# Scores as four products with corrections, k-interleaved starts, later norm statistics and decay copies on ScalarE in a two-layer decoder trunk

## The chip, the cores and the metric

The kernel runs on one core of a Trainium2 chip. The time is the device time of one launch in microseconds (us); runs of the kernel before and of the changed one are compared by their medians. The engines are called TensorE (PE in the rows, PEld its weight loads), VectorE (DVE), ScalarE (ACT), GpSimd (POOL) and SyncE (SP, which here only starts transfers).

## The reference

One inference step of a two-layer trunk on 592 columns: 16 meta tokens, 64 sample tokens (8 sequences of 8) and 512 prompt tokens, with a model width of 1024. Each layer is a mixer and an MLP, each followed by a layer norm. The even mixer runs a state space part (SSD, 16 heads) and a gated recurrence (RG-LRU) side by side; the odd one runs 4 GLA heads and 8 HGRN2 heads. Cut to what the change touches:

```python
# layer norm after each mixer and each MLP
mu = mean(x);  var = mean(square(x - mu))
y = (x - mu) * rsqrt(var + eps) * g + b
# convolution before SSD and RG-LRU, four taps
out = b + sum(full[:, t:t + L] * w[t] for t in range(4))
# SSD, per chunk of 64: decay from cumulated log a
decay = exp(where(causal, b[t] - b[s], -inf))
y_intra = einsum(cb * decay, xd)
# GLA and HGRN2, per chunk c of 64, b = cumsum(log_f)
b_ref = b[:, c // 2]
scores = einsum('tk,sk->ts', q * exp(b - b_ref), k * exp(b_ref - b))
scores = where(causal, scores, 0);  o_intra = scores @ v
S = S * exp(b_last) + (k * exp(b_last - b)).T @ v
# MLP
y = square(relu(h @ w1)) @ w2
```

The kernel takes the GLA and HGRN2 chunks in pairs of 128 tokens, so that one tile of scores holds two reference chunks on its diagonal and one block between them.

## The kernel before

**Tiling.** Activations lie transposed, features on the 128 partitions and the 592 columns along the free axis, cut into two halves of 296 (after the second layer's mixer 288, since the meta columns are dropped). A dense product of 1024 by 1024 is eight k-tiles of 128 by 128 weights for each output tile. For precision each operand is a high and a low fp32r part, and each k-tile costs three matmuls (`mm`, L176 to L186): 24 matmuls for one half of one output tile. Weight tiles come from memory in order; ScalarE casts the high part (L126) and VectorE subtracts the low one (L127). Products of the MLP's second matrix use a two-by-two scheme with fewer multiplications (L195).

**Order.** The program is written as one sequence of `Task`s (L276). A task makes its two halves, its `consume` takes the result out of PSUM, and after each half `weave` (L265) takes every generator in `active` one step further: state space pairs (`pair`, L832), heads (`attend`, L1150) and norms are such generators, so that their small products stand between the large ones. A function in `later[k]` runs after k-tile k of the next product (L184). A scheduling layer then fixes the order on each engine, and each engine works through its own queue in that order. PSUM has five banks for dense products (`pm`) and three for small ones (`px`).

**Norm.** `Norm.add` (L431) takes a finished tile of the residual, squares it on ScalarE and adds it into a sum of squares on VectorE (L447), and the tile itself into a plain sum (L444, the last tile's on VectorE). `finish` puts the statistics of half 0 into `later[FIK]`, with FIK 3, so the two matmuls with a matrix of ones (L463, L465) follow k-tile 3 of the next product; those of half 1 come at once, after `drain`. `finishing` subtracts the mean, scales and writes the high and low part of the next stage's input `h` (L494 to L496).

**Stage starts.** Each MLP starts with four output tiles half by half (`run(..., by_half=True)`, L648), the odd mixer with a 32-wide product for the GLA decay (`lr`), then q, k, v0 and v1 (L1404).

**State space pair.** The convolution has its first tap on VectorE (L706), two more there (L708), the last at L781; ScalarE takes a tanh (L783) and VectorE makes `xs` (L787). `pair` loads its states (`sin`), makes `rr` and `rx`, the per-head log decays spread over masks, on GpSimd (L843, L845), and after steps in between multiplies them into decays on TensorE (L879, L884), exponentiates (L881, L885), and builds inter-chunk outputs and states (L894 to L929).

**Head.** `attend` makes four exponentials of cumulated decays: `e1` (queries), `kx` (keys against the middle of a chunk), `e4` (keys to the chunk's end) and `e3`. Scores of a pair of chunks are two products of 64 query columns (L1265, L1266), the second with keys referred to another point. Then come the 32-wide products of the sample tokens with the states (L1276).

Of the kernel before, what the change touches and what calls it, by code (L numbers as in the profile page):

```python
# [14 lines left out]
P = 128  # L15
# [11 lines left out]
FIK = 3  # L27
# [44 lines left out]
def _trunk(ctx, tc, nc, I, O):  # L72
# [221 lines left out]

    def run(tasks, by_half=False, after=None):
# [99 lines left out]
    class Norm:  # L395
# [3 lines left out]
        def __init__(self, new, rs, halves, gname, bname, layer, final=False):  # L399
            self.rs, self.halves, self.final = rs, halves, final  # L400
            self.gname, self.bname, self.layer = gname, bname, layer
            self.new = new

# [27 lines left out]
        def add(self, k, i):  # L431
# [15 lines left out]
            V.tensor_tensor(ss, ss, q, OP.add)  # L447

        def finish(self, i, dst):
            if i == 0:  # L450
                later.setdefault(FIK, []).append(lambda: step(self.finishing(i, dst)))
            else:
                drain()
                for _ in self.finishing(i, dst):
                    pass

        def finishing(self, i, dst):
            c0, c1 = self.halves[i]
# [88 lines left out]
    def mlp(H, layer, halves, last, keep=None):  # L547
# [3 lines left out]
        with ExitStack() as st:  # L551
# [96 lines left out]
            run([w1(0, f) for f in W1_ORDER[:4]], by_half=True)  # L648
# [27 lines left out]
    def even_mixer(H, g):  # L676
# [10 lines left out]
        def conv_task(i, w, b, done):  # L687
# [3 lines left out]
            def consume(p, c0, c1, half):  # L691
# [14 lines left out]
                V.tensor_scalar(acc[:, 0:OW], t[:, 0:OW], w(0), b, OP.mult, OP.add)  # L706
# [125 lines left out]
        def pair(j, xs, zs, gs):  # L832
# [9 lines left out]
            for i, l in enumerate((lah.bitcast(F32), lal.bitcast(F32))):  # L842
# [6 lines left out]
            yield  # L849
            xd = s2.tile([P, 5, 2, 64], F32, tag="xd", name="xd")  # L850
# [270 lines left out]
    def odd_mixer(H, g):  # L1121
# [28 lines left out]
        def attend(q, k, ls, sc, qs, vf, gate, gcol, sdram, sout, pout, more):  # L1150
# [18 lines left out]

            kx = sd.tile([P, 64 + 4 * 192], F32, tag="kx", name="kx")  # L1170
            kc = kx[:, 64:].rearrange("p (c r s) -> p c r s", c=4, r=3)
# [6 lines left out]
            V.tensor_tensor(kc[:, :, 1], b4[:, :, 96:97].to_broadcast([P, 4, 64]), b4[:, :, 0:64], OP.subtract)  # L1178
            c = slice(16, 592)
            A.activation(kx[:, 0:64], e1[:, 16:80], AF.Exp, scale=-sc)  # L1180
            A.activation(kc[:, :, 0:3:2], e1[:, 80:592].rearrange("p (c r s) -> p c r s", c=4, r=2), AF.Exp, scale=-sc)
            A.activation(e1[:, c], e1[:, c], AF.Exp, scale=sc)
            A.activation(e4, e4, AF.Exp, scale=sc)
            A.activation(kc[:, :, 1], kc[:, :, 1], AF.Exp, scale=sc)
# [14 lines left out]
            k4 = k[:, 80:592].rearrange("p (c r s) -> p c r s", c=4, r=2)  # L1199
            V.tensor_tensor(kx[:, 0:64], k[:, 16:80], kx[:, 0:64], OP.mult)  # L1200
            V.tensor_tensor(kc[:, :, 0:2], k4[:, :, 0:1].to_broadcast([P, 4, 2, 64]), kc[:, :, 0:2], OP.mult)
            V.tensor_tensor(kc[:, :, 2], k4[:, :, 1], kc[:, :, 2], OP.mult)
            V.tensor_tensor(e4, k, e4, OP.mult)
            for j in range(2):
# [55 lines left out]

            p = px()
# [8 lines left out]
            p = px()  # L1270
            if nv == 2:
                samples(p[:, 256:512])
# [350 lines left out]
```

## Time and profile before

| | before |
|---|---|
| median of 3 runs | 1928.42 us (1928.1 to 1928.71) |
| profiled execution | 1926.06 us, span 1924.3 us |
| TensorE busy | 1858.2 us, 97% |
| VectorE busy | 1297.1 us, 67% |
| ScalarE busy | 886.0 us, 46% |
| GpSimd busy | 417.2 us, 22% |
| granted TensorE clock, mean | 0.987 |
| chain that ended last | PE 80%, DVE 13%, ACT 3%, issue 3% |

A share of busy time is a mean over stages with different limits. By the clock of the span, the state space part fills about 0 to 260 us, RG-LRU 260 to 380, the first output product and norm to 485, the first MLP to 893, the odd mixer to 1420, its output product and norm to 1510, the second MLP to 1908, and the last norm and stores the rest. "Idle" of an instruction is the time that its engine stood still just before it, and the arrow names what ended that. PEclk is the clock granted to TensorE as a share of its full 2.4 GHz; 0.50 is its other level, 1.2 GHz.

### The profile page before, as it was taken

The page shows a single profiled execution, that of the slowest core. Times are in us where ns is not written, and L with a number is a line of the kernel's source. Part 1 is how long each engine was busy: PE and PEld are TensorE (multiplying, and loading weights), DVE is VectorE, ACT ScalarE, POOL GpSimd, SP SyncE. Part 2 cuts the span into 40 slices and gives each one's busy share as a digit, 9 for nine tenths or more (in the row PEclk, how much of TensorE's full clock was granted, in tenths as well). Part 3 has the DMA queues.
Part 4 walks back from the last instruction along what each step waited for, and adds up shares of the span by engine and source line. Part 5 has one row for each costly group of instructions (what it writes and reads, how often), then busy time and mean ns, then how long its engine had stood idle before and what let it go on. Part 6 is the DMA issues. An engine that isn't in the chain of part 4 may idle for free.

```text
span 1924.3 us, 33593 instructions
## 1 busy us (share of the span) xinstructions
PE 1858.2 (97%) x13854; PEld 1819.0 (95%) x13854; DVE 1297.1 (67%) x2035; ACT 886.0 (46%) x1550; POOL 417.2 (22%) x435
## 2 busy tenths in 40 slices
PE   8998899999999999998999999999999999999996
PEld 8998799899999999998999999999999999999996
DVE  7997766877975756549645465665755976666647
ACT  5333246623644444324644455665732653534333
POOL 2554432214100000035422222221203200000024
PEclk9999899999999999999999999999999999999998
DMA  6232221421213131322332233223231214141311
GB/s 205 91 114 72 75 100 47 132 88 47 87 56 120 46 127 48 122 76 72 132 113 104 100 104 106 84 90 102 91 126 56 77 56 132 46 131 55 122 55 50
DMA packets 68761, 175.97 MB, mean 91 GB/s; under 512 B 6624, under 2 KB 30304, under 8 KB 67456
## 3 DMA queue, kind: packets, MB, share of 16 engines
q1 hardware_dynamic: 67968, 171.40, 26.5%
q8 instruction: 109, 1.79, 0.4%
q0 software_dynamic: 640, 2.43, 0.4%
q14 instruction: 44, 0.36, 0.1%
HBM read 154.54 MB, written 19.25 MB: 90 GB/s over the span
## 4 chain that ended last, share of the span: by engine, by line
PE 80%; DVE 13%; ACT 3%; issue 3%; POOL 0%; DMA 0%; SPq 0%; ACTq 0%; DVEq 0%; POOLq 0%
PE pm L182 55%; PE pm L195 14%; DVE w L127 1%; DVE r L424 1%; DVE h L496 1%; DVE r L494 1%; PE px L1326 1%; DVE r L478 1%; PE px L1337 1%; PE px L1336 1%; PE px L1067 1%; DVE lnq L447 1%; DVE acc L708 1%; PE px L925 1%; DVE ln L447 1%
## 5 line engine op out<-in xcount | busy, mean ns | idle before, releaser
L182 PE MATMUL pm<-h,w 128*128 128x296 f32 (+2 forms) x8256 | 1178.2, 301 | 11.0 <-ACT h L308 5.4
L182 PEld LDWEIGHTS pm<-h,w 128*128 128x128 f32 x8256 | 1132.6, 189 | 22.6 <-ACT h L308 5.4
L127 DVE TENSOR_TENSOR w<-raw,w 128x1024 fp32r<-128x1024 f32 (+1 forms) x300 | 369.7, 1233 | 165.1 <-ACT w L126 164.5
L126 ACT CAST w<-raw 128x1024 fp32r<-128x1024 f32 (+1 forms) x300 | 304.2, 1015 | 301.6 <-PE pm L195 152.2
L195 PE MATMUL pm<-ff,w 128*128 128x296 f32 (+1 forms) x2016 | 273.3, 297 | 0.0
L195 PEld LDWEIGHTS pm<-ff,w 128*128 128x128 f32 x2016 | 271.9, 188 | 0.1
L620 POOL TENSOR_TENSOR sq<-sq 128x296 f32<-128x296 f32 (+1 forms) x32 | 21.5, 674 | 651.4 <-ACT sq L618 651.4
L182 PE MATMUL pm<-m,w 128*128 128x296 f32 (+1 forms) x768 | 108.2, 304 | 0.0
L182 PE MATMUL pm<-ff,w 128*128 128x296 f32 (+1 forms) x768 | 108.0, 303 | 0.0
L182 PEld LDWEIGHTS pm<-m,w 128*128 128x128 f32 x768 | 106.8, 194 | 0.8 <-issue 0.3
L182 PEld LDWEIGHTS pm<-ff,w 128*128 128x128 f32 x768 | 106.6, 193 | 0.8 <-issue 0.3
L607 DVE TENSOR_TENSOR ff<-sq,ff 128x888 fp32r<-128x888 f32 (+3 forms) x48 | 58.4, 1221 | 42.1 <-ACT ff L606 42.1
L588 ACT ACTIVATE sq<-pm 128x296 f32<-128x296 f32 (+1 forms) x96 | 37.9, 414 | 87.0 <-PE pm L182 66.0
L606 ACT CAST ff<-sq 128x888 fp32r<-128x888 f32 (+3 forms) x48 | 50.3, 1050 | 39.6 <-DVE sq L601 38.9
L1361 POOL TENSOR_TENSOR o<-o,zs 128x576 f32<-128x576 f32 x16 | 31.3, 1967 | 148.7 <-DVE o L1360 148.7
L1280 POOL TENSOR_TENSOR sin<-sin,ebl 128x1024 f32<-128x1024 f32 (+1 forms) x12 | 35.8, 2980 | 106.1 <-issue 101.2
L211 DVE TENSOR_TENSOR r<-r,pm 128x296 f32<-128x296 f32 (+1 forms) x96 | 43.5, 453 | 18.6 <-PE pm L195 18.0
L589 ACT ACTIVATE sq<-sq 128x296 f32<-128x296 f32 (+1 forms) x96 | 41.2, 450 | 0.8
L1366 ACT COPY v<-pm 128x296 f32<-128x296 f32 x32 | 12.9, 405 | 58.6 <-PE pm L182 58.6
L214 DVE TENSOR_TENSOR r<-r,pm 128x296 f32<-128x296 f32 (+1 forms) x72 | 32.6, 452 | 10.2 <-PE pm L195 10.2
L618 ACT ACTIVATE sq<-pm 128x296 f32<-128x296 f32 (+1 forms) x32 | 13.0, 414 | 56.8 <-PE pm L182 53.8
L495 ACT ACTIVATE h<-r,vec 128x296 fp32r<-128x296 f32 (+1 forms) x48 | 23.8, 536 | 31.5 <-DVE r L494 31.5
(390 smaller groups left out, 2261.3 us busy)
## 6 DMA issues: line engine op xcount, KB each, us to landing
raw<-in_w_dram SPq DMA_DIRECT2D x252, 512.0 KB, 3.3
sin<-in_sst_dram SPq DMA_DIRECT2D x8, 512.0 KB, 3.7
out_ssd_s_dram<-sin SPq DMA_DIRECT2D x8, 512.0 KB, 3.1
sin<-in_gst_dram SPq DMA_DIRECT2D x4, 1024.0 KB, 5.7
out_gla_s_dram<-sin SPq DMA_DIRECT2D x4, 1024.0 KB, 3.9
sin<-in_hst_dram SPq DMA_DIRECT2D x8, 512.0 KB, 4.4
out_hgrn_s_dram<-sin SPq DMA_DIRECT2D x8, 512.0 KB, 3.5
xt<-in_x_dram SPq DMA_DIRECT2D x16, 148.0 KB, 4.2
```

The costliest lines, as they stand in the source:

```text
L126: A.copy(w[:, 0, :n], r)
L127: V.tensor_tensor(w[:, 1, :n], r, w[:, 0, :n].bitcast(F32), OP.subtract)
L182: PE.matmul(p[:, :n], w[:, a, ks], xs[k][:, b, c0:c1], start=(k == 0 and i == 0), stop=(k == KT - 1 and i == 2))
L195: PE.matmul(p[:, :n], w[:, a, ks], xs[k][:, b, :n], start=(first and k == 0 and i == 0), stop=(k == 3 and i == 2), skip_group_check=True)
L211: V.tensor_tensor(y, y, p[:, :n], OP.add)
L214: V.tensor_tensor(y, y, p[:, :n], OP.subtract)
L447: V.tensor_tensor(ss, ss, q, OP.add)
L588: A.activation(q, p, AF.Relu)
L589: A.activation(q, q, AF.Square)
L606: A.copy(t[:, 0, a:e, :n], s[:, a + 1:e + 1, :n])
L607: V.tensor_tensor(t[:, 1, a:e, :n], s[:, a + 1:e + 1, :n], t[:, 0, a:e, :n].bitcast(F32), OP.subtract)
L1280: G.tensor_tensor(sin, sin, ebl[:, 0:8].unsqueeze(2).to_broadcast([P, 8, N]), OP.mult)
```

## The change

Seven edits:

1. FIK is 6, so the statistics of half 0 come three k-tiles, nine matmuls, later in the next product.
2. `together` takes up to four tasks through the k-tiles side by side, one PSUM bank each: at the start of an MLP, and at the start of the odd mixer, where `lr`, q, k and v0 share one run.
3. The addition of a square into the sum of squares is put off until the next tile comes (`add_square`).
4. Half 1's `finish` prepares one more weight unit ahead of `drain`.
5. The first tap of the convolution goes from VectorE to ScalarE (20 times).
6. The spread log decays of a pair go from four GpSimd instructions to twenty ScalarE copies with a per-partition scale, eight before the first `yield` of the pair and twelve after.
7. The scores of a head are four products of 128 query columns with one set of keys, and four 64 by 64 ones that write the second chunk's own upper block anew with keys of the other reference point; the transposes of the samples come ahead of them, and key exponentials and products are fewer and longer.

```diff
-FIK = 3
+FIK = 6
...
+    def together(tasks, i):
+        ps = []
+        for t in tasks:
+            if t.small is None and t.w is None:
+                t.w = next_unit()
+            ps.append(pm())
+        for k in range(KT):
+            ks = slice(k * P, (k + 1) * P)
+            for t, p in zip(tasks, ps):
+                c0, c1 = t.halves[i]
+                if t.small is not None:
+                    ops = [(p[:32], t.small[:, k, :], b) for b in range(2)]
+                else:
+                    ops = [(p, t.w[:, a, ks], b) for a, b in ((0, 0), (0, 1), (1, 0))]
+                for j, (o, w, b) in enumerate(ops):
+                    PE.matmul(o[:, :c1 - c0], w, t.xs[k][:, b, c0:c1], start=(k == 0 and j == 0),
+                              stop=(k == KT - 1 and j == len(ops) - 1))
+            for fn in later.pop(k, ()):
+                fn()
...
-            V.tensor_tensor(ss, ss, q, OP.add)
+            self.add_square()
+            self.square = (ss, q)
...
+                prep_to(state["use"] + 4)
                 drain()
...
-            run([w1(0, f) for f in W1_ORDER[:4]], by_half=True)
+            ts = [w1(0, f) for f in W1_ORDER[:4]]
+            together(ts, 0)
+            together(ts[:2], 1)
+            together(ts[2:], 1)
...
-                V.tensor_scalar(acc[:, 0:OW], t[:, 0:OW], w(0), b, OP.mult, OP.add)
+                A.activation(acc[:, 0:OW], t[:, 0:OW], AF.Identity, scale=w(0), bias=b)
...
-                G.tensor_tensor(rr[:, i], l[:, 1:5, hh].unsqueeze(3).to_broadcast([P, 4, 2, P]),
-                                umask[:, None, None, :].to_broadcast([P, 4, 2, P]), OP.mult)
-                G.tensor_tensor(rx[:, i], l[:, 0, hh].unsqueeze(2).to_broadcast([P, 2, 80]),
-                                uxmask[:, None, 0:80].to_broadcast([P, 2, 80]), OP.mult)
+            def decays(m):
+                for i, l in enumerate((lah.bitcast(F32), lal.bitcast(F32))):
+                    for h in range(2):
+                        def scaled(out, mask, c):
+                            A.activation(out, mask, AF.Copy, scale=l[:, c, 2 * j + h:2 * j + h + 1])
+                        if m == 2:
+                            scaled(rx[:, i, h], uxmask[:, 0:80], 0)
+                        else:
+                            for c in (2 * m, 2 * m + 1):
+                                scaled(rr[:, i, c, h], umask, c + 1)
...
-                o = 64 + c * 192
-                PE.matmul(p[:, c * P:c * P + 64], kx[:, o:o + P], e1[:, a:a + 64], start=True, stop=True)
-                PE.matmul(p[:, c * P + 64:(c + 1) * P], kx[:, o + 64:o + 192], e1[:, a + 64:b], start=True, stop=True)
+                PE.matmul(p[:, c * P:(c + 1) * P], kx[:, a - 16:b - 16], e1[:, a:b], start=True, stop=True)
+            for c in range(4):
+                a, b = ptiles(c + 1)
+                PE.matmul(p[0:64, c * P + 64:(c + 1) * P], k2[:, c], e1[:, a + 64:b], start=True, stop=True)
...
-                run([Task(H, FULL, lr_consume, small=wsr[:, 1])] + tasks[0:NB], by_half=True)
-                run(tasks[NB:])
+                ts = [Task(H, FULL, lr_consume, small=wsr[:, 1])] + tasks
+                together(ts[:4], 0)
+                ts[4].half(0)
+                together(ts[:2], 1)
+                together(ts[2:4], 1)
+                ts[4].half(1)
```

What this makes of the queues shows at three places. On TensorE, at the first output product's norm and the start of the first MLP (`m` is the product's input, `lns` and `lnq` the sums, `ones` the matrix of ones), the order before was

```order
L182 MATMUL pm<-m_4612,w 128x296 x3
L182 MATMUL pm<-m_4615,w 128x296 x3
L182 MATMUL pm<-h,w 128x296 x25
L463 MATMUL px<-lns,ones 128x296
L465 MATMUL px<-lnq,ones 128x296
L182 MATMUL pm<-h,w 128x296 x455
```

and it is now

```order
L182 MATMUL pm<-m_4743,w 128x296 x3
L311 MATMUL pm<-h,w 128x296 x32
L500 MATMUL px<-lns,ones 128x296
L311 MATMUL pm<-h,w 128x296 x7
L502 MATMUL px<-lnq,ones 128x296
L311 MATMUL pm<-h,w 128x296 x153
```

The statistics of half 1 stood after 25 matmuls of the MLP and stand after 32 and 39 of the interleaved ones now; those of half 0, further up, moved nine matmuls down.

On ScalarE, in the state space part near 190 us of the old span, the queue before (`de` and `dx` are exponentials of decays, the instruction on `pad` is the tanh ahead of `xs`) read

```order
L702 COPY pad<-pm 128x296
L126 CAST w<-raw 128x1024
L881 ACTIVATE de<-px 128x512 x2
L885 ACTIVATE dx<-px 128x160
L783 ACTIVATE pad<-acc 128x616
L984 ACTIVATE zs<-pm 128x296
L848 COPY xr<-xs 128x240
L984 ACTIVATE zs<-pm 128x296
```

and now reads

```order
L742 COPY pad<-pm 128x296
L126 CAST w<-raw 128x1024
L746 ACTIVATE acc<-pad,hcb,hcw 128x616
L932 ACTIVATE de<-px 128x512 x2
L936 ACTIVATE dx<-px 128x160
L888 ACTIVATE rr<-msk,lah 128x128 x4
L888 ACTIVATE rr<-msk,lal 128x128 x4
L888 ACTIVATE rr<-msk,lah 128x128 x3
L823 ACTIVATE pad<-acc 128x616
L888 ACTIVATE rr<-msk,lah 128x128
L1035 ACTIVATE zs<-pm 128x296
```

The first tap stands behind a weight cast now, and eleven of a later pair's copies stand ahead of the tanh; the other nine come after it.

On TensorE, at the scores of one HGRN2 head, the queue was

```order
L1266 MATMUL px<-e_11768,kx 128x64
L1265 MATMUL px<-e_11768,kx 128x64
L1266 MATMUL px<-e_11768,kx 128x64
L1265 MATMUL px<-e_11768,kx 128x64
L1266 MATMUL px<-e_11768,kx 128x64
L1276 MATMUL px<-sin,qm_9327 32x128 x8
```

with eight score products in all, and is

```order
L182 MATMUL pm<-h,w 128x280 x24
L1314 MATMUL px<-e_11888,kx 128x128 x4
L1317 MATMUL px<-e_11888,kx 64x64 x4
L1325 MATMUL px<-sin,qm_9460 32x128 x8
L182 MATMUL pm<-h,w 128x296 x24
```

Eight products of 64 columns became four of 128 columns and four of 64 columns and 64 wide.

## Rows read from the trace of the kernel before

**Rows 1.** Busy time of TensorE, share of the span, instructions; the same of its weight loads.

```profile
PE 1858.2 (97%) x13854; PEld 1819.0 (95%) x13854; DVE 1297.1 (67%) x2035; ACT 886.0 (46%) x1550; POOL 417.2 (22%) x435
```

**Rows 2.** Waits of TensorE: line, releaser, us in total, times, longest us.

```profile
PE px L918 <- DVE yi L897: 9.8, 3, 4.9
PE px L463 <- DVE ln L444: 8.2, 3, 3.5
PE px L463 <- DVE lns L444: 6.9, 2, 3.5
...
PE px L925 <- DVE S L911: 4.6, 3, 2.2
...
PE px L1067 <- DVE xr L1055: 2.8, 1, 2.8
PE px L1247 <- DVE e L1203: 1.9, 1, 1.9
```

**Rows 3.** Timeline of TensorE, state space part: start us, us, instruction, idle, releaser.

```profile
192.72 2.33 PE L182 MATMUL pm<-h,w 128*128 128x296 f32 x16
197.37 0.89 PE L918 MATMUL px<-xsr,bmx 120*128 120x128 f32 x6 [2.32 <-DVE yi L897]
```

**Rows 4.** Timeline of VectorE, the same stretch.

```profile
186.73 2.51 DVE L708 SCALAR_TENSOR_TENSOR acc<-pad,hcw,acc 128x616 f32<-128x616 f32 x1
...
194.38 2.50 DVE L781 SCALAR_TENSOR_TENSOR acc<-pad,hcw,acc 128x616 f32<-128x616 f32 x1
...
197.04 0.28 DVE L897 TENSOR_TENSOR yi<-px,ex 128x128 f32<-128x128 f32 x1
```

**Rows 5.** Timeline of GpSimd, the same stretch.

```profile
189.52 2.88 POOL L843 TENSOR_TENSOR rr<-lal,msk 128x1024 fp32r<-128x1024 f32 x1
...
193.33 2.89 POOL L899 TENSOR_TENSOR sin<-sin,ex 128x1024 f32<-128x1024 f32 x1
```

**Rows 6.** Timeline of ScalarE, the same stretch.

```profile
196.97 0.72 ACT L783 ACTIVATE pad<-acc 128x616 f32<-128x616 f32 x1 [8.79 <-DVE acc L781]
```

**Rows 7.** Stretches: bounds, length, busy us of each engine, PEclk, DMA share, GB/s.

```profile
196.00:200.00 4.00, 1.11 (x8) 0.97 (x8) 3.79 (x14) 2.67 (x5) 0.47 (x3) 1.00 0.01 2
200.00:204.00 4.00, 3.31 (x16) 3.34 (x17) 3.85 (x8) 0.00 (x0) 0.00 (x0) 0.57 0.15 38
227.00:235.00 8.00, 6.84 (x31) 6.87 (x32) 4.32 (x11) 0.18 (x1) 0.00 (x0) 0.57 0.45 141
463.00:470.00 7.00, 6.38 (x22) 5.76 (x23) 2.45 (x5) 3.95 (x7) 2.44 (x4) 0.52 0.01 2
875.00:880.00 5.00, 4.46 (x17) 3.97 (x18) 3.32 (x6) 2.07 (x5) 2.65 (x3) 0.66 0.01 3
...
1890.00:1897.00 7.00, 6.19 (x23) 5.62 (x24) 4.90 (x9) 2.04 (x5) 3.73 (x4) 0.53 0.00 0
```

**Rows 8.** Costliest groups, then single lines: ns at least, median, most.

```profile
L126 ACT CAST w<-raw 128x1024 fp32r<-128x1024 f32 (+1 forms) x300 | 304.2, 1015 | 301.6 <-PE pm L195 152.2
...
L708 DVE SCALAR_TENSOR_TENSOR acc<-pad,hcw,acc x24: 846/854/2514, 22.4 to 218.0; 128x616 f32<-128x616 f32 x24
...
L1426 ACT ACTIVATE ls<-k,lbt x8: 881/882/884, 1118.0 to 1362.3; 128x592 f32<-128x592 f32 x8
...
L1224 ACT COPY vs<-px x12: 246/268/373, 954.5 to 1393.5; 128x128 f32<-128x128 f32 x8, 128x256 f32<-128x256 f32 x4
```

**Rows 9.** Timeline of TensorE ahead of a norm's statistics.

```profile
856.18 15.85 PE L182 MATMUL pm<-ff,w 128*128 128x296 f32 x114
```

**Rows 10.** Timeline of TensorE, scores of one HGRN2 head, then narrow products.

```profile
1219.97 0.33 PE L1265 MATMUL px<-e,kx 128*128 128x64 f32 x2
...
1221.48 0.39 PE L1266 MATMUL px<-e,kx 128*128 128x64 f32 x2
1221.80 0.65 PE L1276 MATMUL px<-sin,qm 128*32 128x128 f32 x16
...
180.40 1.04 PE L948 MATMUL px<-de,xd 128*64 128x128 f32 x16
```

More of the change, by code (lines that the diff above doesn't have):

```diff
@@ L293, in half @@
             weave()
+    def together(tasks, i):
[17 more added lines that the diff above has]
+                fn()
+        for t, p in zip(tasks, ps):
+            c0, c1 = t.halves[i]
+            t.consume(p[:32 if t.small is not None else P, :c1 - c0], c0, c1, i)
+            flush()
+            weave()
     def run(tasks, by_half=False, after=None):
@@ L402, in __init__ @@
             self.new = new
+            self.square = None
         def shift(self):
@@ L446, in add, with add_square @@
             A.activation(q, r, AF.Square)
-            V.tensor_tensor(ss, ss, q, OP.add)
+            self.add_square()
+            self.square = (ss, q)
+        def add_square(self):
+            if self.square:
+                ss, q = self.square
+                V.tensor_tensor(ss, ss, q, OP.add)
+            self.square = None
         def finish(self, i, dst):
@@ L457, in finishing @@
         def finishing(self, i, dst):
+            self.add_square()
             c0, c1 = self.halves[i]
@@ L841, in pair @@
             rx = s1.tile([P, 2, 2, 80], F32R, tag="rx", name="rx")
-            for i, l in enumerate((lah.bitcast(F32), lal.bitcast(F32))):
-                G.tensor_tensor(rr[:, i], l[:, 1:5, hh].unsqueeze(3).to_broadcast([P, 4, 2, P]),
-                                umask[:, None, None, :].to_broadcast([P, 4, 2, P]), OP.mult)
-                G.tensor_tensor(rx[:, i], l[:, 0, hh].unsqueeze(2).to_broadcast([P, 2, 80]),
-                                uxmask[:, None, 0:80].to_broadcast([P, 2, 80]), OP.mult)
+            def decays(m):
[8 more added lines that the diff above has]
+                                scaled(rr[:, i, c, h], umask, c + 1)
+            decays(0)
             xr = s1.tile([P, 2, 3, 40], F32, tag="xr", name="xr")
@@ L849, in pair @@
             yield
+            decays(1)
+            decays(2)
             xd = s2.tile([P, 5, 2, 64], F32, tag="xd", name="xd")
@@ L1167, in attend @@
             e1, e4 = (g(n) for n in ("e1", "e4"))
-            kx = sd.tile([P, 64 + 4 * 192], F32, tag="kx", name="kx")
-            kc = kx[:, 64:].rearrange("p (c r s) -> p c r s", c=4, r=3)
+            kx = sd.tile([P, 576 + 256], F32, tag="kx", name="kx")
+            k2 = kx[:, 576:].rearrange("p (c s) -> p c s", c=4)
             for o, s, r in zip(chunks(e1, 64), chunks(bs, 64), (4, 32)):
@@ L1177, in attend @@
             b4 = chunks(bs, 128)[1]
-            V.tensor_tensor(kc[:, :, 1], b4[:, :, 96:97].to_broadcast([P, 4, 64]), b4[:, :, 0:64], OP.subtract)
+            V.tensor_tensor(k2, b4[:, :, 96:97].to_broadcast([P, 4, 64]), b4[:, :, 0:64], OP.subtract)
             c = slice(16, 592)
-            A.activation(kx[:, 0:64], e1[:, 16:80], AF.Exp, scale=-sc)
-            A.activation(kc[:, :, 0:3:2], e1[:, 80:592].rearrange("p (c r s) -> p c r s", c=4, r=2), AF.Exp, scale=-sc)
+            A.activation(kx[:, 0:576], e1[:, c], AF.Exp, scale=-sc)
             A.activation(e1[:, c], e1[:, c], AF.Exp, scale=sc)
             A.activation(e4, e4, AF.Exp, scale=sc)
-            A.activation(kc[:, :, 1], kc[:, :, 1], AF.Exp, scale=sc)
+            A.activation(k2, k2, AF.Exp, scale=sc)
             e3 = bs
@@ L1198, in attend @@
             V.scalar_tensor_tensor(e1[:, c], q[:, c], qs, e1[:, c], OP.mult, OP.mult)
[L1199 to L1202, printed above, removed]
+            V.tensor_tensor(kx[:, 0:576], k[:, c], kx[:, 0:576], OP.mult)
             V.tensor_tensor(e4, k, e4, OP.mult)
+            V.tensor_tensor(k2, chunks(k, 128)[1][:, :, 0:64], k2, OP.mult)
             for j in range(2):
@@ L1259, in attend @@
             yield
+            u = px()
+            if nv == 2:
+                samples(u[:, 256:512])
             p = px()
```

4 lines of the change are left out of this document (1 added, 3 removed).

## The prediction

> **What bounds the kernel now.** I read the shares of the engines first: TensorE is busy 1858.2 us, 97% of the span [rows 1], so the time can fall only where TensorE stands still, runs at its lower clock, or gets fewer or shorter products. The waits of TensorE say where it stands still [rows 2]: in the state space part 9.8 us in three waits at L918 and 4.6 at L925, each behind a VectorE instruction; ahead of the norms' statistics 8.2 and 6.9 us at L463, which are four waits of about 3.5 us and a last one of 1.2 that belongs to the final norm's second half; 2.8 at L1067 in RG-LRU; 1.9 at L1247 in the last head. Then the stretches with their granted clock [rows 7]. Around those waits it is 0.57 (200 to 204 us, 227 to 235), 0.52 at the first norm, 0.66 at the second (the third reads the same, 0.66 over 5 us), 0.53 at the last, a mix of the full 2.4 GHz and the level of 1.2. Length times what is missing from 1.00 is what the lower clock costs: 4 x 0.43 + 8 x 0.43 = 5.1 us in the state space part, 7 x 0.48 + 5 x 0.34 + 5 x 0.34 + 7 x 0.47 = 10.1 us at the norms (a little less, as part of it is idle anyway). So each of these waits costs up to twice its length. But the stretch of 196 to 200 us, with a wait of 2.32 us in front of it and in it [rows 3], shows 1.00 [rows 7]: the clock fell only when a second wait followed.
>
> **The decays and the first tap, state space part.** In the stretch at 190 us, TensorE is done with L182 at 192.72 + 2.33 = 195.05 and starts L918 at 197.37, released by `yi` of L897 [rows 3], which VectorE ran at 197.04, behind the taps L708 of 2.51 us and L781 of 2.50 [rows 4]. Alone such a tap takes 0.85 [rows 8]. The slow ones lie beside GpSimd's L843, 2.88 us, and L899, 2.89 [rows 5]. The change takes L843 and L845 off GpSimd, while L899 stays. Two L708 at 0.85 for 2.5 give 3.3 us; with L781 as well it would be 4.95. Against it, the first tap now comes later: it takes 0.88 on ScalarE (nearest row, a 592-column activation with both pointers, L1426) where VectorE spent at most a tap's 0.85, and stands behind a weight cast of 1.0 us (L126) [rows 8]; that is 1.0 to 1.9 us. So `yi` comes 1.4 (3.3 less 1.9) to 4.0 us (4.95 less 1.0) earlier, and the wait of 2.32 goes, or leaves 0.9; I take 2.0 of it. L925's wait, for the state `S` made behind `yi`, is 2.2 here [rows 2]; both ends move up, VectorE's by some 1 us more, so I leave 1.2 of it. With the clock at 1.00 the 1.7 us of that window come back: 2.0 + 1.0 + 1.7 = 4.7. The stretch at 220 us has the same pattern: its waits are about 2.5 (9.8 less 4.9 and 2.3) and 2.2, its clock loss 3.4, so 2.2 + 1.0 + 3.4 = 6.6. The longest wait, 4.9 us at 170, ends in the same `yi`, but stands behind the group's norm on VectorE and the ScalarE work in front of that; I give it 1 at most, and the taps on ScalarE may take it back. Sum 12.3, taken as 12. Bounds: 4, if L781 beside L899 and the late first tap eat the rest and the clock falls all the same; 17, with 4.9 gone too and the clock kept.
>
> The twenty copies of a pair have as nearest row a 128x128 copy without a pointer, 0.25 us (L1224) [rows 8]; with starts a little apart that is 20 x 0.27 = 5.4 us a pair, 43 in all eight. ScalarE stood idle 8.79 us ahead of the tanh at 196.97 [rows 6], and the eleven copies that the new queue puts there fill 3.0 of them. I cost them at nothing on that cover. If it is gone, each microsecond of them lands on `xs` and on everything behind.
>
> **Norms.** Nine more matmuls ahead of the statistics take 9 x 15.85 / 114 = 1.25 us [rows 9] out of each wait of 3.5, four times 5.0 us in all; 2.2 us of each wait stay, as the sum of VectorE comes no earlier: the new queue still has the square's addition ahead of the last tile's, so the putting off gains 0 to 0.4. After a single wait of 2.3 the clock stayed [rows 3, 7], so I take the 10.1 us back as well. What is late next is `h`: the next stage starts at the same tile, but its first products want four banks and all of `h` sooner, and half 1's statistics stand between its matmuls. For that I take off 2. The odd start changes between 32 and 128 wide sixteen times where it did once; a narrowing cost 0.10 us, as 1221.48 to 1221.80 is 0.32 for a product of 0.22 [rows 10], so 1.8 with a little for the way back. 5.0 + 10.1 - 2 - 1.8 = 11.3; bounds 5 (no clock back) and 18 (waits gone).
>
> **Scores.** Before, 1221.80 - 1219.97 = 1.83 us a head for eight products, 0.22 each and 0.10 for the step to 32 wide [rows 10]. A product of 64 columns had two records as one of 128 has, so I take 0.22 for the wide ones too: 0.88. The four of 64 by 64 are nearest to L948, 1.04 us for eight, 0.13 each [rows 10]: 0.52. With two narrowings 0.10 each, 1.60: 0.23 less, twelve times 2.8, taken as 3. Bounds: -1.6 when a small one costs 0.22 (0.36 more each head), 5.4 when it overlaps fully.
>
> The Trainium skill ("TensorEngine Tiling (Array Packing)", Key Properties) says that a change of the tiling mode drains TensorE. The rows show a pause only on the way to the narrower mode; by the rule each way would count, and the change would lose another 0.1 us for each of the 16 returns and 12 heads, 3 us in all, an estimate from the row's 0.10.
>
> **The rest.** `e4`'s product now comes before the long key product, so L1247's 1.9 us go but for 0.4: 1.5 (0 to 1.9). L1067's wait of 2.8 [rows 2] stands behind taps on VectorE, of which the first is gone, at most 0.85; I take 0.6 (0 to 2.8, where ScalarE brings the tap late or the whole wait goes). The weight unit prepared earlier I cost at nothing; it keeps to the place of `drain`.
>
> Sum: 12 + 11.3 + 3 + 1.5 + 0.6 = 28.4. From the profiled execution's 1926.06 that is 1897.7; the median of the runs stands 2.4 above that execution, so **1900 us**.
>
> **Rivals.** First, the norms give nothing: the wait moves from the statistics to the banks and to `h`, and the clock falls there. For it: four banks of five are taken by one bundle while VectorE still has half 1's residual additions to do. Then 28.4 - 11.3 = 17 us, 1911. Second, more goes: all 14.4 us of waits and 5.1 of clock in the state space part, and the norms' whole 14 and 10, plus 5: 48 us, 1880. Against it, VectorE's chains at 170 us and behind the last tile are untouched. Third, slower: the copies on ScalarE are exposed. ScalarE takes its queue in order; if a copy takes 0.5 us rather than 0.27, or the tanh ahead of `xs` becomes ready before the copies ahead of it are done in all eight pairs, up to 10 us a pair stand on the path. From 28.4 / 8 = 3.6 us a pair it is slower than before; at 5.4 in each of eight it is 43 - 28 = 15 slower, 1943. Against it stand the 8.79 us of idle time [rows 6]. The Trainium skill ("ScalarE: Activation LUTs", What ACT_TABLE_LOAD costs) puts 93 ns on each pointer operand; a copy would then be 0.34 us and the eleven 3.7, by my estimate, still within that idle time. Fourth, the putting off of the squares is undone by the scheduler; the queue shows that it is at the last tiles, and it is costed so.
>
> **How the numbers follow.** Forecast 0.60, norms without gain 0.18, more than forecast 0.10, copies exposed 0.08, a mix of small losses near no change 0.04. The range reaches from the second rival's side to the first one's: bounds summed half way, 4 to 12 of the state space part and no norm gain give 1914 (28.4 less 11.3 less 3 = 14 us); 17, 18, 5 and 2 give 1886. A measurement of this kernel can tell 0.2%, 3.9 us, from no change. Faster by more 0.88, within 0.04, slower 0.08.
>
> **What would show it.** Right: L708's median stays 0.85 and its longest falls below 1.5; waits at L918 of the old code fall under 7 us with the clock near 1.00 between 195 and 235; the statistics' waits are about 2.2 us and the clock after them is 1.00; scores take 1.6 us a head. Wrong: a ScalarE wait ahead of `xs`; a new wait at the first bundle of an MLP with the clock at 0.5; narrow products of 0.22.

## The result and the profile after

The changed kernel took 1903.43 us (median of 4 runs, 1900.32 to 1905.49), the one before 1928.26 (4 runs): a ratio of 0.9872 with a 95% interval of 0.9854 to 0.9889, or 24.8 us less. 1900 us had been forecast, with a range of 1886 to 1914. The profiled execution is the slowest of the four, 1905.49 us, with a span of 1903.7; against the span before that is 20.6 us.

TensorE's waits after, as line, releaser, us in total, times, longest us:

```profile
PE pm L311 <- DVE r L556: 6.7, 5, 1.7
...
PE px L500 <- DVE ln L471: 4.4, 3, 1.5
PE pm L311 <- DVE r L671: 3.8, 2, 2.4
PE px L500 <- DVE lns L471: 2.9, 2, 1.5
PE px L1118 <- DVE xr L1106: 2.6, 1, 2.6
PE px L969 <- DVE yi L948: 2.5, 1, 2.5
PE px L976 <- DVE S L962: 2.5, 2, 1.2
PE pm L311 <- ACT sq L625: 2.4, 2, 1.4
PE px L1294 <- DVE e L1249: 1.5, 1, 1.5
```

L969 and L976 are what L918 and L925 were, L500 is L463, L1118 is L1067, L1294 is L1247 [rows 2]. At `yi` and `S` in the state space part 14.4 us of waits became 5.0, at the statistics 15.1 became 7.3. L311 are the interleaved products at the stage starts. They wait 6.7 + 3.8 us for residual additions on VectorE (L556, L671), which hand back PSUM banks, 2.4 for an activation ahead of the squares (L625), and 1.8 in smaller pieces, 14.7 in all. The starts waited before too, for `h` and not for banks:

```profile
PE pm L182 <- DVE h L496: 3.0, 4, 1.1
...
PE pm L247 <- DVE h L496: 1.7, 2, 1.3
...
PE pm L182 <- ACT h L495: 1.6, 2, 0.8
...
PE pm L247 <- ACT h L495: 0.7, 1, 0.7
```

That is 7.0 us, and 7.5 with one for `lgf` of the odd start. So the statistics lost 7.8 us of waits, and the starts gained 7.2.

The stretch that stood at 190 us [rows 3 to 6] is now, on VectorE,

```profile
186.22 0.85 DVE L748 SCALAR_TENSOR_TENSOR acc<-pad,hcw,acc 128x616 f32<-128x616 f32 x1
...
188.12 0.85 DVE L748 SCALAR_TENSOR_TENSOR acc<-pad,hcw,acc 128x616 f32<-128x616 f32 x1
188.89 2.04 DVE L938 TENSOR_TENSOR dx<-dx,cbx 128x160 f32<-128x160 f32 x1
190.86 0.85 DVE L821 SCALAR_TENSOR_TENSOR acc<-pad,hcw,acc 128x616 f32<-128x616 f32 x1
191.63 0.28 DVE L948 TENSOR_TENSOR yi<-px,ex 128x128 f32<-128x128 f32 x1
```

and on GpSimd

```profile
188.75 1.99 POOL L950 TENSOR_TENSOR sin<-sin,ex 128x1024 f32<-128x1024 f32 x1 [4.41 <-PE px L945]
```

The two taps L748 and the last one, L821, take 0.85 us again. GpSimd's scaling of the states, L950, is still there, but the instruction beside it is now L938, 2.04 us where its median is 0.32. `yi` comes at 191.63, not 197.04. On ScalarE eleven copies lie ahead of the tanh L823 and are done before it could start:

```profile
186.88 1.28 ACT L888 ACTIVATE rr<-msk,lah 128x128 fp32r<-128x128 f32 x4
188.05 1.27 ACT L888 ACTIVATE rr<-msk,lal 128x128 fp32r<-128x128 f32 x4
189.22 0.98 ACT L888 ACTIVATE rr<-msk,lah 128x128 fp32r<-128x128 f32 x3
191.82 0.72 ACT L823 ACTIVATE pad<-acc 128x616 f32<-128x616 f32 x1 [1.61 <-DVE acc L821]
```

Four copies take 1.17 us from the start of one group to that of the next; eleven of them, 3.2 us, fit, and the tanh still waits 1.61 us for VectorE.

Stretches with the granted clock (before the last two columns) that answer to [rows 7]: the two of the state space part, then the starts of the first MLP, the odd mixer and the second MLP.

```profile
192.00:200.00 8.00, 6.77 (x55) 6.66 (x54) 6.40 (x18) 5.20 (x17) 0.26 (x3) 1.00 0.14 32
214.00:222.00 8.00, 6.77 (x53) 6.66 (x53) 6.79 (x20) 5.02 (x14) 0.25 (x2) 1.00 0.11 23
462.00:475.00 13.00, 9.64 (x56) 8.99 (x55) 12.23 (x23) 6.63 (x14) 2.87 (x3) 0.87 0.13 45
876.00:887.00 11.00, 7.22 (x32) 6.25 (x32) 9.15 (x20) 4.75 (x10) 2.55 (x3) 0.69 0.22 80
1488.00:1498.00 10.00, 8.33 (x38) 7.87 (x39) 7.83 (x16) 3.87 (x9) 2.36 (x3) 0.66 0.15 52
```

The first two are at full clock. At the three starts the clock is still a mix with its lower level: 13 x 0.13 + 11 x 0.31 + 10 x 0.34 = 8.5 us lost, where 10.1 were lost around the statistics before. What TensorE waits for at the first MLP:

```profile
466.85 1.33 PE L311 MATMUL pm<-h,w 128*128 128x296 f32 x8 [1.61 <-DVE r L556]
469.93 4.10 PE L311 MATMUL pm<-h,w 128*128 128x296 f32 x18 [1.75 <-DVE r L556]
...
487.63 2.59 PE L311 MATMUL pm<-h,w 128*128 128x296 f32 x17 [1.35 <-ACT sq L625]
```

And the scores of one head, to be held against [rows 10]:

```profile
1204.86 1.05 PE L1314 MATMUL px<-e,kx 128*128 128x128 f32 x8
1205.84 0.68 PE L1317 MATMUL px<-e,kx 128*64 128x64 f32 x8
1206.45 0.64 PE L1325 MATMUL px<-sin,qm 128*32 128x128 f32 x16
```

The four wide products and the step to 64 wide take 0.98 us, the four narrow ones and the step to 32 wide 0.61: 1.59 us a head, for 1.83.

**Where the time went.** The first start of an instruction that both kernels have dates each stage (lines by the old numbers): the recurrence's first L1067 (286.08 us before, 272.74 after), the norms' first matmuls L421 (443.51 and 430.13; 855.41 and 841.32; 1470.19 and 1452.07; 1871.17 and 1856.20), the first head's 32-wide product L1276 (954.96 and 940.74).

| stage | forecast | measured |
|---|---|---|
| state space part | -12 | -13.3 |
| RG-LRU, first output product | -0.6 | 0.0 |
| first norm and MLP | | -0.7 |
| second norm, odd start, to the first head's 32-wide product | | -0.1 |
| heads to the third norm | -4.5 (scores 3, last head 1.5) | -3.9 |
| third norm and second MLP | | +3.2 |
| last norm and the end | | -5.6 |
| the four rows without a forecast, all norms and starts | -11.3 | -3.3 |

The scores' part of the stages after the second norm is 12 x 0.24 = 2.9 us. So the state space part and the scores came as forecast, and the norms gave less than a third in this execution.

One execution is not the whole answer, since the clock moves such a row by some microseconds. The row with the second MLP is 404.1 us here and 404.0 in x7, but 401.1, 401.3 and 401.2 in x2, x6 and x8, which have the same code there; before it was 401.0. In x6 and x7, whose code is that of the changed kernel at all four norms, the last row of the table reads -5.8 and -3.5. So the norms gave 3 to 6 us.

### The profile page after: what moved, and what is told of

Read it like the earlier page. It is cut to its first block, busy times and chain, and to the rows that moved or that the text cites. A ratio compares the mean times of both kernels' runs of the same rounds, so it can differ in the third digit from the quotient of the medians.

```text
span 1903.7 us, 33716 instructions
## 1 busy us (share of the span) xinstructions
PE 1851.3 (97%) x13854; PEld 1811.8 (95%) x13854; DVE 1258.1 (66%) x2003; ACT 942.5 (50%) x1718; POOL 362.6 (19%) x403
## 4 chain that ended last, share of the span: by engine, by line
PE 81%; DVE 13%; ACT 3%; issue 3%; POOL 0%; DMA 0%; ACTq 0%; DVEq 0%
PE pm L182 54%; PE pm L195 14%; PE pm L311 3%; DVE w L127 2%; DVE r L515 1%; DVE r L531 1%; DVE h L533 1%; DVE r L451 1%; PE px L1375 1%; DVE acc L748 1%; PE px L1386 1%; PE px L1385 1%; PE px L1118 1%; ACT w L126 1%; PE px L1314 1%
## 5 line engine op out<-in xcount | busy, mean ns | idle before, releaser
L182 PE MATMUL pm<-h,w 128*128 128x296 f32 (+2 forms) x7728 | 1102.7, 301 | 6.2 <-ACT h L334 5.5
L311 PE MATMUL pm<-h,w 128*128 128x296 f32 (+1 forms) x528 | 84.9, 319 | 13.6 <-DVE r L556 6.7
L311 PEld LDWEIGHTS pm<-h,w 128*128 128x128 f32 x528 | 79.5, 205 | 18.2 <-ACT h L532 12.2
L625 ACT ACTIVATE sq<-pm 128x296 f32<-128x296 f32 (+1 forms) x96 | 37.3, 413 | 88.0 <-PE pm L182 66.3
L1410 POOL TENSOR_TENSOR o<-o,zs 128x576 f32<-128x576 f32 x16 | 30.8, 1936 | 152.0 <-DVE o L1409 152.0
L211 DVE TENSOR_TENSOR r<-r,pm 128x296 f32<-128x296 f32 (+1 forms) x96 | 43.5, 453 | 18.6 <-PE pm L195 17.9
L1329 POOL TENSOR_TENSOR sin<-sin,ebl 128x1024 f32<-128x1024 f32 (+1 forms) x12 | 31.2, 2598 | 97.9 <-issue 93.2
L1415 ACT COPY v<-pm 128x296 f32<-128x296 f32 x32 | 12.9, 406 | 56.7 <-PE pm L182 56.7
```

Source lines behind the costliest of these rows:

```text
L182: PE.matmul(p[:, :n], w[:, a, ks], xs[k][:, b, c0:c1], start=(k == 0 and i == 0), stop=(k == KT - 1 and i == 2))
L211: V.tensor_tensor(y, y, p[:, :n], OP.add)
L311: PE.matmul(o[:, :c1 - c0], w, t.xs[k][:, b, c0:c1], start=(k == 0 and j == 0), stop=(k == KT - 1 and j == len(ops) - 1))
L625: A.activation(q, p, AF.Relu)
L1329: G.tensor_tensor(sin, sin, ebl[:, 0:8].unsqueeze(2).to_broadcast([P, 8, N]), OP.mult)
L1410: G.tensor_tensor(o[v][:, c], o[v][:, c], gate[v][:, c], OP.mult)
```

## The experiments

Three questions: where the norms' gain went, whether the state space part's gain is the decays' or the first tap's, and whether the scores cost what the rows said. All twelve kernels are the changed one with one or more edits; "the changed kernel" is 1903.43 us, ratio 0.9872. Ratios are to runs of the kernel before on the same chip, and their intervals reach 0.0013 to 0.0018 to either side.

**x1, MLP starts half by half.**

```diff
-            together(ts, 0)
-            together(ts[:2], 1)
-            together(ts[2:], 1)
+            run(ts, by_half=True)
```

> The changed kernel with both MLP starts half by half as before; the odd start stays interleaved. Banks theory: the interleaved start of four products waits for PSUM banks that VectorE still holds (1.6 + 1.75 + 1.35 us at the first MLP, 1.6 + 1.6 + 0.5 + 1.1 at the second) and drops the clock; half by half these go, some 2 us of waits for h come instead at each, the clock stays: 5 to 8 us faster than the changed kernel. Rival, late statistics: h comes 1.25 us later with FIK 6, so the waits for h fill the same gap, 3 us or more at each MLP, and the clock falls too: within 2 us of the changed kernel.

Measured: 1902.92 us, ratio 0.9869 (0.9854 to 0.9883). No difference. The waits of L311 at the MLPs, 9.6 us, are gone; waits for `h` came instead, 3.6 and 1.8 us in twelve pieces. The most of them:

```profile
PE pm L182 <- ACT h L532: 3.6, 5, 0.9
```

**x2, odd start half by half.**

```diff
-                together(ts[:4], 0)
-                ts[4].half(0)
-                together(ts[:2], 1)
-                together(ts[2:4], 1)
-                ts[4].half(1)
+                run(ts, by_half=True)
```

> The changed kernel with the odd mixer's start half by half as before; the MLP starts stay interleaved. Banks theory: the waits of 1.35 + 2.4 us for VectorE's residual additions and the clock at half speed after them (about 3 us lost) go, with 1.8 us of changes between 32 and 128 wide; waits for h of 2 to 3 us come back: 4 us faster. Rival: h is the limit, and the waits for it are as long as those for banks: no difference beyond 1.5 us.

Measured: 1904.28 us, ratio 0.9874 (0.9859 to 0.9889). No difference either. The rivals' times hold in both: interleaving four products neither wins nor loses against going half by half.

**x3, statistics after k-tile 3.**

```diff
-FIK = 6
+FIK = 3
```

> The changed kernel with the statistics of half 0 after k-tile 3 again. Forecast's view: each of four waits grows from 1.5 by 1.25 us and the clock falls for 4 to 6 us after each, 5 + 8 us; h comes 1.25 us earlier, which takes back some 1 us at each of three starts: 8 to 12 us slower than the changed kernel. Rival, late statistics: what is won at the statistics is lost at the next start: within 3 us.

Measured: 1902.52 us, ratio 0.9863 (0.9847 to 0.9880). No difference, as the rival has it. The statistics' waits grew from 7.3 to 12.4 us in all, as expected, and the starts gave back 2.6 of it (L311 waits 12.1 us for 14.7). The other 2.5 are less than the spread of the runs. With starts that interleave four products, no gain of the later statistics shows.

**x4, three products interleaved at the MLPs.**

```diff
-            together(ts, 0)
-            together(ts[:2], 1)
-            together(ts[2:], 1)
+            together(ts[:3], 0)
+            ts[3].half(0)
+            for t in ts:
+                t.half(1)
```

> The changed kernel with three products interleaved at an MLP's start, then the fourth, then half 1 product by product. Banks theory: one bank less to wait for, the wait of 1.75 us at the fourth bank goes and that of 1.35 for a burst of squares too: 3 to 6 us faster than the changed kernel, and as fast as or faster than half by half, as the k-tiles still ask for h more slowly. Rival, late statistics: h's waits replace them, within 2 us.

Measured: 1898.73 us (1895.73 to 1900.67), ratio 0.9846 (0.9829 to 0.9862), 4.7 us less than the changed kernel; the intervals overlap a little. The time is what the banks theory has, but the profiled execution is the fastest of the four, and 3.5 us of its lead are the clock elsewhere (last section), so x10 to x12 had to confirm it.

**x6, decays on GpSimd again.**

```diff
-            def decays(m):
...
-            decays(0)
+            for i, l in enumerate((lah.bitcast(F32), lal.bitcast(F32))):
+                G.tensor_tensor(rr[:, i], l[:, 1:5, hh].unsqueeze(3).to_broadcast([P, 4, 2, P]),
...
-            decays(1)
-            decays(2)
```

> The changed kernel with the spread decays on GpSimd again, the first tap left on ScalarE. Port theory (the forecast's): taps of 2.5 us beside GpSimd come back on VectorE, the waits of 2.3 and 2.2 us at 190 and 220 us and the low clock after them too, and the late first tap adds to them: the state space part ends 12 to 15 us later, 1915 to 1918 us in all. Rival, tap theory: what helped was the first tap off VectorE: 2 to 4 us slower only. Second rival, copies cost: without 160 copies ScalarE is free and it is not slower.

Measured: 1917.52 us, ratio 0.9940 (0.9926 to 0.9953), 14.1 us more than the changed kernel, with intervals apart. This is what the first of the three views has: the longest tap is 2.5 us again, the waits at 200 us are back, and those at 228 us with 2.38 and 1.42. That the taps are long beside these GpSimd instructions is shown; that a port is the reason is not, as no run tells it from another one.

```profile
L748 DVE SCALAR_TENSOR_TENSOR acc<-pad,hcw,acc x24: 759/854/2499, 24.2 to 224.0; 128x616 f32<-128x616 f32 x24
```

```profile
200.36 1.94 PE L959 MATMUL px<-xsr,bmx 120*128 120x128 f32 x8 [2.37 <-DVE yi L938]
203.74 2.05 PE L966 MATMUL px<-S,bc 128*128 128x128 f32 x8 [1.45 <-DVE S L952]
```

**x7, first tap on VectorE again.**

```diff
-                A.activation(acc[:, 0:OW], t[:, 0:OW], AF.Identity, scale=w(0), bias=b)
+                V.tensor_scalar(acc[:, 0:OW], t[:, 0:OW], w(0), b, OP.mult, OP.add)
```

> The changed kernel with the first tap of the convolutions on VectorE again, decays left on ScalarE. Port theory: the tap is neutral in the state space part, as it waits behind a weight cast on ScalarE for what it saves on VectorE; L1118's wait in RG-LRU stays 2.6: within 2 us of the changed kernel. Rival, tap theory: VectorE is what is short there, so 12 taps of 0.6 us come back: 5 us slower.

Measured: 1899.91 us (1899.29 to 1900.98), ratio 0.9852 (0.9839 to 0.9866), 3.5 us less than the changed kernel, by itself inside the intervals. Neither theory: the tap on ScalarE costs. The traces carry it: the first L1118 starts at 268.30 us for 272.74, and everything behind is as before. It comes after a weight cast there, so `xs` comes late in each of the first pairs. TensorE in the changed kernel, and then in x7, at the transposes of `xs` of the same pair:

```profile
99.18 0.63 PE L908 MATMUL px<-msk,xs 128*128 128x128 f32 x4 [0.32 <-DVE xs L827]
```

```profile
97.91 0.66 PE L908 MATMUL px<-msk,xs 128*128 128x128 f32 x4
```

From one pair to the next these transposes are 99.18 - 77.42 = 21.8 us apart in the changed kernel and 97.91 - 76.89 = 21.0 in x7. Of the 4.4 us, 1.7 are waits of TensorE (13.9 us before that L1118 in the changed kernel, 12.2 in x7), and 1.7 more are the clock at 170 us, which is 0.79 over 8 us in x7 where it was 0.58 (last section); the last 1.0 is not placed:

```profile
168.00:176.00 8.00, 7.50 (x58) 7.33 (x58) 4.04 (x8) 1.09 (x4) 0.21 (x1) 0.79 0.51 187
```

It is 0.79 there in x11, x12 and x13 too, the other runs with this edit.

**x8, scores of before.** The edit puts L1170 to L1184, L1199 to L1203 and L1261 to L1272 of the kernel before back.

```diff
-                PE.matmul(p[:, c * P:(c + 1) * P], kx[:, a - 16:b - 16], e1[:, a:b], start=True, stop=True)
-            for c in range(4):
-                a, b = ptiles(c + 1)
-                PE.matmul(p[0:64, c * P + 64:(c + 1) * P], k2[:, c], e1[:, a + 64:b], start=True, stop=True)
+                o = 64 + c * 192
+                PE.matmul(p[:, c * P:c * P + 64], kx[:, o:o + P], e1[:, a:a + 64], start=True, stop=True)
+                PE.matmul(p[:, c * P + 64:(c + 1) * P], kx[:, o + 64:o + 192], e1[:, a + 64:b], start=True, stop=True)
```

> The changed kernel with the scores and key exponentials of before. By the trace a head's scores took 1.59 us for 1.83, twelve heads 2.9 us, and the wait ahead of the last head's transposes of e4 grows from 1.5 to 1.9: 3 to 4 us slower than the changed kernel. Rival: the drain of the mode changes eats it, within 1 us.

Measured: 1906.30 us, ratio 0.9883 (0.9870 to 0.9897), 2.9 us more. As 12 x 0.24 has it, but by itself inside the intervals; the traces carry it, with 1.59 for 1.83 us a head. From the first head's 32-wide product to the third norm, x8 takes 515.3 us, the kernel before 515.2 and the changed one 511.3, all three at full clock.

**x10, three interleaved at all starts.** x4's edit, and at the odd start

```diff
-                together(ts[:4], 0)
-                ts[4].half(0)
-                together(ts[:2], 1)
-                together(ts[2:4], 1)
-                ts[4].half(1)
+                together(ts[:3], 0)
+                ts[3].half(0)
+                ts[4].half(0)
+                for t in ts:
+                    t.half(1)
```

> The changed kernel with three products interleaved at all three starts (at the odd one lr, q and k), the rest one by one. Banks theory: as with three at the MLPs alone (1898.7 us), and at the odd start the wait of 2.4 us for the fourth bank goes and half as many changes of width: another 1 to 4 us, 1895 to 1898. Rival: the odd start waits for h, 1899 as without it.

Measured: 1896.98 us (1892.79 to 1899.55), ratio 0.9835 (0.9818 to 0.9851): 6.5 us less than the changed kernel, with intervals apart. That this start is better than four at once is shown. How is another matter: the waits for banks fall from 12.9 us to 4.6, but those at the statistics rise from 7.3 to 14.0.

```profile
PE px L500 <- DVE lns L471: 7.0, 4, 2.2
PE px L500 <- DVE ln L471: 7.0, 4, 2.5
...
PE pm L311 <- DVE r L556: 3.3, 3, 1.6
...
PE pm L311 <- DVE r L671: 1.3, 1, 1.3
```

At the first MLP, the 1.75 us that the fourth product waited for its bank are now 2.18 us ahead of half 1's statistics, again for VectorE. All waits of TensorE together are 38.0 us for 40.4. The larger part is the clock: its mean is 0.991 to 0.996 in the four runs, for 0.989 to 0.992 in those of the changed kernel, and 0.003 of 1900 us are 6 us.

**x11, x10 with the first tap on VectorE.** The edits of x10 and x7.

> The changed kernel with three products interleaved at all three starts and the first tap on VectorE: the two edits that were faster alone (1897.0 and 1899.9 for 1903.4). They touch different stages; if they add up, 1893 to 1895. If the late tap only changed how the clock fell in those runs, no better than 1897.

Measured: 1893.96 us (1893.37 to 1894.81), ratio 0.9821 (0.9806 to 0.9836). They add up; this is the fastest kernel of the study, 9.5 us ahead of the changed one.

**x12, x11 with the statistics after k-tile 3.** The edit of x3 on x11.

> The same (three interleaved, tap on VectorE) with the statistics of half 0 after k-tile 3. Queue theory: VectorE's queue between two stages is what is short, and h, sums and banks only share its delay; with one bank less to wait for, earlier statistics are again worth as much as later ones cost: within 2 us of the run with FIK 6. Forecast's view: waits of 2.7 for 1.5 us at four statistics and the clock falling there: 5 us or more slower.

Measured: 1903.86 us (1902.15 to 1904.66), ratio 0.9871 (0.9856 to 0.9885), 9.9 us more than x11 on the same chip. Here the forecast's view holds in time: with three interleaved the later statistics are worth something. The same lines and the stretch after the first norm's half 0, in x11, then in x12:

```profile
PE px L500 <- DVE lns L471: 7.0, 4, 2.1
PE px L500 <- DVE ln L471: 6.9, 4, 2.5
```

```profile
444.00:452.00 8.00, 6.93 (x47) 6.64 (x48) 6.00 (x11) 5.58 (x9) 3.44 (x4) 1.00 0.13 42
```

```profile
PE px L500 <- DVE lns L471: 11.0, 4, 3.1
PE px L500 <- DVE ln L471: 10.0, 4, 3.3
```

```profile
444.00:452.00 8.00, 6.56 (x33) 5.94 (x34) 4.22 (x8) 4.31 (x7) 2.81 (x5) 0.79 0.01 3
```

The waits for sums rise from 13.9 to 21.0 us, but those at the starts fall from 6.0 to 1.3, so all waits of TensorE are 39.2 us for 36.9. As to waits, the queue theory has it about right. What it left out is the clock. At half 0's statistics TensorE waits 2.6 to 2.7 us in x12 and 1.4 to 1.5 in x11, and over the 8 us around it the clock reads 0.79 at all four norms of x12 and 1.00 at all four of x11. Four times 8 x 0.21 are 6.7 us; with 2.3 of waits that is 9.0 of the 9.9, an estimate.

**x13, part of h's low half on GpSimd.** On x11, for tiles 3, 5 and 7:

```diff
+                    if k in (3, 5, 7):
+                        A.activation(r, r, AF.Identity, bias=b)
+                        G.tensor_tensor(dst[k][:, 1, c0:c1], r, dst[k][:, 0, c0:c1].bitcast(F32), OP.subtract)
```

> The same (three interleaved, tap on VectorE, FIK 6) with the low part of h for tiles 3, 5 and 7 made by ScalarE (one more activation) and GpSimd in place of VectorE. Queue theory: 1.5 us less of VectorE's queue in each half of three norms, the residual additions behind them come earlier, waits for banks and h fall by 1 to 1.5 us at each start: 2 to 5 us faster. Rival, port: GpSimd's instruction holds VectorE up for as long as it takes off: within 1 us, or slower.

Measured: 1904.23 us (1903.00 to 1905.52), ratio 0.9874 (0.9859 to 0.9889), 10.3 us more than x11. Slower, as the rival allows, though a port is not what the waits name: each of GpSimd's 18 instructions takes about 1.0 us, the odd start stands 3.1 us for one of them (L535), and the sums come later too (L500 waits 18.1 us for x11's 13.9). From the second norm to the first head's 32-wide product it takes 105.4 us for x11's 97.7, so most of the loss is at the odd start. The queue theory is not tested by this run: it did not shorten the path to `h`.

**x14, squares added at once, no earlier weight unit.**

```diff
-            self.add_square()
-            self.square = (ss, q)
+            V.tensor_tensor(ss, ss, q, OP.add)
...
-                prep_to(state["use"] + 4)
```

> The changed kernel without the putting off of the squares and without the earlier weight unit (both costed at nothing). Forecast: within 1.5 us of the changed kernel. Rival: the earlier unit puts a subtraction of 1.2 us into VectorE's queue ahead of h, so without it 2 us faster; or the putting off spares VectorE the wait for ScalarE's squares, so without it 3 us slower.

Measured: 1905.76 us (1904.08 to 1907.11), ratio 0.9879 (0.9861 to 0.9897), 2.3 us more than the changed kernel, inside the intervals. The statistics' waits are 10.5 us in it for 7.3, those of L311 12.1 for 14.7: another wait that mostly moves. The two edits were not separated.

## Why the prediction held, and where it was off

**State space part: right.** 12 us were forecast, 13.3 measured, and x6 puts 14.1 us on the decays. Of the eight traces that have this part's code, seven put its end at 272.4 to 273.0 us, and x4 at 269.2, where the clock did not fall at 170. The taps L748 fell to 0.85 as the step said, and L821 too, since L950 meets L938 instead, the favourable end of the step. The wait for `yi` went at 190 and 220 us, that for `S` left 1.2 each, the figure forecast. At 170 us the wait fell from 4.9 to 2.5, 2.4 us where 1 at most had been given. What the sum did not have about cancels: two waits near the start of the part (L818 and L822, 3.4 us) fell to 0.6, and new ones for `xs` (L908), `yi` (L993) and `de` (L945) came to 2.2.

**The first tap: the sign was wrong.** The step had it 1.0 to 1.9 us late in the stretches that waited already, covered there, and gave L1067 0.6 us of gain; L1118 waits 2.6 for 2.8, and over the kernel the tap costs 3.5 us (x7). The step did not look at the first pairs, which did not wait for `xs` before and now do, three times 0.3 us, with the pairs 0.7 us further apart; about as much again is the clock at 170 us. The queue rows ahead of the prediction show the cause, the tap behind a weight cast.

**The copies on ScalarE: right.** Costed at nothing on a cover of 8.79 us of idle time; the trace shows 3.2 us used of it and 1.61 still idle.

**Norms: the term that was mis-sized**, 11.3 forecast, 3.3 measured in the profiled execution and 3 to 6 with x6 and x7. Its first half held: the waits at the statistics fell from about 3.5 to 1.5 us, even more than the 1.25 of nine matmuls, and the clock after them stayed full (after the first, until 468 us). What failed is the cost at the next start, for which 2 us were taken off. The starts had no slack: they waited 7.0 us for `h` already, which the prediction's reading of the waits left out, and VectorE was busy there, after, for 12.23 of 13 us at the first (the third busy time of its row). So of the 7.8 us of waits that the statistics gained, the starts lost 7.2, and the clock falls there instead. That was the first rival, priced at 1911, and one of the signs of being wrong, a new wait at the first bundle of an MLP; it came true at the three norms with a start behind them, while the last norm, which has none, gave 5.6 us.

The 1.8 us taken off for the changes of width at the odd start came to nothing as well. In these lines the 32-wide products and the others all start 0.13 to 0.14 us apart, in both directions:

```profile
887.75 1.38 PE L311 MATMUL pm<-h,w 128*128 128x280 f32 x9
888.97 0.43 PE L311 MATMUL pm<-h,wsr 128*32 128x296 f32 x2
889.24 1.36 PE L311 MATMUL pm<-h,w 128*128 128x280 f32 x9
```

x3 shows the trade from the other side: earlier statistics cost nothing that can be told from the spread. x12 shows that it hung on the starts: with three products interleaved in place of four (and the tap on VectorE), later statistics are worth 9.9 us, 2.3 of them in waits and most of the rest in clock. That TensorE meets the same queue of VectorE at the banks, at `h` and at the sums is read from the releasers of the waits (L556, L671, L533, L471); no run changed the number of banks alone. What the runs leave open is why the waits at some places bring the clock down and at others do not.

**Scores: right.** 1.60 us a head was forecast, 1.59 measured, by its parts: 0.98 is four times 0.22 and 0.10, and 0.61 four times 0.13 and 0.10. x8 gives 2.9 us for the whole. The rule of the Trainium skill ("TensorEngine Tiling (Array Packing)", Key Properties) that a change of the tiling mode drains TensorE shows as 0.10 us on each step to a narrower mode. It shows on the way back too, which the prediction did not see and which lies outside these sums: behind the 32-wide products the first wide one starts at 1207.02 us and the second 0.23 later, where 0.13 is usual. The kernel before has the same (1222.37 and 1222.60 us), once a head as here, so the 3 us of the prediction's estimate did not come.

**Last head: mis-sized.** 1.5 us was forecast and 0.4 came: L1294 waits 1.5 us where L1247 waited 1.9. `e4`'s product does stand behind one key product where it stood behind three. What the step did not see is that GpSimd's instruction of 1.9 us, which lay beside the key products (L1361), lies beside `e4`'s own now (L1410). The product took 0.76 us before (L1203), and takes 1.98 after:

```profile
1368.74 1.98 DVE L1249 TENSOR_TENSOR e<-k,e 128x592 f32<-128x592 f32 x1
```

```profile
1368.23 1.86 POOL L1410 TENSOR_TENSOR o<-o,zs 128x576 f32<-128x576 f32 x1 [5.50 <-DVE o L1409]
```

**The sum.** 28.4 us were forecast, and between the two profiled executions it is 20.6: the state space part gave 1.3 more, the norms 8.0 less, L1067 and the heads 0.6 less each. By the medians it is 24.8. That the median lies within 3.4 us of the forecast is in part luck: the profiled execution before stands 2.2 us below its median, the one after 2.1 above. In the four runs time and mean granted clock go together: 1905.49 and 1904.63 us at 0.989, 1902.24 at 0.991, 1900.32 at 0.992.

## What to carry to other kernels

A wait behind a queue that is itself short of time moves when its place in the order changes; before a gain is booked, look at what the same queue hands out next, PSUM banks above all. In this kernel asking for three at once in place of four was better by 6.5 us. Work moved to an engine with free time costs nothing only where it does not stand behind that engine's long instructions in the queue; look also at the places that did not wait before. A sum of waits is not the whole price: x10 and x12 change it by 2 us and the time by 6.5 and 9.9, so the granted clock is to be read beside it. Interactions are large: the same edit (statistics three k-tiles later) was worth nothing with one start and 9.9 us with another, so edits are tested together as well as alone.

## What the runs showed of the hardware

The clock does not fall at the same wait in every run. The changed kernel and x4 have the same code up to the first MLP, and the same wait of 2.49 us for `yi`; in the changed kernel's trace the clock fell after it, in x4's it did not, and the part up to RG-LRU's first L1118 took 272.74 us in the one and 269.21 in the other:

```profile
169.29 1.97 PE L969 MATMUL px<-xsr,bmx 120*128 120x128 f32 x8 [2.49 <-DVE yi L948]
```

```profile
168.00:176.00 8.00, 6.71 (x29) 6.71 (x30) 5.69 (x18) 3.00 (x9) 0.73 (x1) 0.58 0.20 75
```

```profile
168.59 1.11 PE L970 MATMUL px<-xsr,bmx 120*128 120x128 f32 x8 [2.49 <-DVE yi L949]
```

```profile
168.00:176.00 8.00, 7.32 (x67) 6.81 (x68) 5.95 (x17) 2.83 (x10) 0.24 (x2) 1.00 0.35 115
```

The traces of x1, x2, x3, x8, x10 and x14 have the same wait, and in each the clock fell (0.57 to 0.61 over these 8 us). So what the prediction took from one place, that the clock stays after a single wait of 2.3 us, does not hold at every place. The difference is 3.5 us, of a spread of 5 us between runs of the changed kernel; so terms of 2 or 3 us are read from medians, from waits and from several traces, not from one trace's stages.

A VectorE instruction beside a long GpSimd one can take longer by more than a microsecond: a tap 2.51 for 0.85 us beside L843 [rows 4, 5], L938 2.04 for 0.32 beside L950's 1.99, and L1249 1.98 beside L1410's 1.86, where its counterpart L1203 took 0.76.

A ScalarE copy of 128x128 with a scale pointer into an fp32r tile takes 0.40 us of busy time (medians of two groups of 64: 411 and 403 ns), and four start within 1.17 us, 0.29 each; the prediction had taken 0.27, and 0.34 in its third rival.
